# Value and gate projection of a gated recurrence: three products of 256 columns per weight block become one of 512 and one of 256

## The chip, the cores and the metric

The kernel runs on one core of one Trainium2 chip. A core has five engines that run their own instruction queues side by side: TensorE (PE in the profile; its weight loads are listed apart as PEld), VectorE (DVE), ScalarE (ACT), GpSimd (POOL) and SyncE (SP), which here issues most of the DMAs. The metric is the time of one execution on the device in microseconds (us). The kernel before takes 2153.63 us, the median of three runs (2153.37 to 2154.8 us).

## The reference, cut to what matters

The program is a two-layer decoder trunk on 1024 tokens of width 1024, all in float32: a gated linear recurrence (HGRN2) with 8 heads of 128, a gated convolutional feed-forward block, sliding-window attention, and a second feed-forward block. The change is in the first part alone. Of it the reference computes

```python
q, f, i, g = jnp.split(h @ w_in, 4, axis=-1)          # each (B, S, 1024): 8 heads of 128
fg = lb + (1.0 - lb) * jax.nn.sigmoid(heads(f))
o = hgrn2_chunkwise(jax.nn.silu(heads(q)), 1.0 - fg, heads(i), jnp.log(fg))   # i is the value
o = o * lax.rsqrt(jnp.mean(jnp.square(o), -1, keepdims=True) + RMS_EPS)
o = o * g_norm_w * jax.nn.silu(heads(g))              # g is the output gate
```

The two products that matter here are the value `i` and the gate `g`: for each head, 1024 tokens by 1024 inputs by 2 x 128 columns. The gate is used as g times sigmoid(g).

## The kernel before, in words

**Products in three parts.** A float32 operand is held as a high part (rounded to the type fp32r that TensorE reads) and a low part (the rest). A product is made of three matmuls into one accumulating bank of PSUM: high by high, high by low, low by high. That is `mm3` (L193 to L197): the matmul of L194 has the high part of the stationary operand and the high part of the moving one, L195 the high part and the low part, L196 the low part and the high part. Each matmul loads its stationary operand anew. The activations, transposed, stand in `T` (index 0 the high, 1 the low part); the weights stand in slots of `HL`. `split_raw` (L180) makes a slot from a loaded tile `raw`: ScalarE casts the high part (L176), then the low part is a subtraction (L169), on VectorE unless said otherwise.

**Value and gate.** For head h, `ig_block(h, us, tp)` (L673) makes value and gate of two blocks of 128 tokens. `us` are two weight tiles, each with four blocks of 128 inputs by 256 columns (128 of value, 128 of gate), high and low part one after the other. `proj_tok` (L213) goes over the two token blocks and the eight input blocks: the activations are stationary (128 by 128), the weights move (256 columns), so that one bank of 512 columns holds value and gate of two token blocks. Then ScalarE takes the sigmoid of the gate (L681) and copies the value to SBUF (L682), and VectorE multiplies sigmoid and gate (L684), reading PSUM. The tiles `V` and `G` have two buffers each; the recurrence of head h uses those of head h - 1 as scratch (L932).

**Order of the work.** The instructions of all engines are put in order by hand in this stage. A small class `Order` keeps a model time `od.t` of TensorE (each `mm3` adds 3n/2365 us) and a model `od.v` of when VectorE is done. Work other than the projections is written as generators; `od.tick()`, called after each `mm3`, steps those that are due, and then lets `lay` (L1060) fill VectorE with low parts and with sums of feed-forward weights (L1108) as long as its model stands less than 1.5 us ahead. A head has eight slots: four of `qf` (L819; 24 matmuls of 512 columns each) and four of `ig_block`. `recur` (L848), the recurrence of one head, is spread over some 50 us of other work: elementwise updates on VectorE (L918 to L923), copies on ScalarE (L905, L906), and small bursts of matmuls (L200).

At the beginning of each slot, `slot_begin` (L1083) puts all low parts still waiting and all gate products still waiting (`soon`) into VectorE's queue. At its end, `slot_end` (L1112) issues the casts of the next weights and registers their low parts. So the low parts go into VectorE's queue right behind the cast that they need, and the gate products right behind their sigmoid. The weights that are loaded wait for a free one of three `raw` tiles, on SP's queue. PSUM has four banks for the projections (`psmm`) and two tiles of two banks for the recurrence (`psax`).

After head 7, TensorE goes on with the output projection (`out_part`, L297), for which `Y_to_T` splits the finished heads into `T`; the last steps of the last recurrence lie between.

Of the kernel before, what the change touches and what calls it, by code (L numbers as in the profile page):

```python
# [107 lines left out]
def trunk(ctx: ExitStack, tc: tile.TileContext, a: dict, out: bass.AP):  # L108
# [31 lines left out]
    def psmm():  # L140
        return mmp.tile([P, 512], F32, name="psmm")
# [511 lines left out]
    with tc.tile_pool(name="t", bufs=1, reuse_waits="tile") as raws, hgrn_pool as hp:  # L653
# [14 lines left out]
        def qf_split(raw, eng=None):  # L668
            return split_raw(raw, eng).rearrange("p h (k c) -> p h k c", k=KC)

        VG = {-1: tuple(hp.tile([P, NB, P], F32, name=n, bufs=2) for n in "VG")}

        def ig_block(h, us, tp, soon=None):  # L673
            if tp == 0:
                VG[h] = (hp.tile([P, NB, P], F32, name="V", bufs=2), hp.tile([P, NB, P], F32, name="G", bufs=2))
            V, G = VG[h]
            ps = psmm()
            proj_tok(us, tp, ps)
            pv = ps.rearrange("p (t g c) -> p t g c", t=2, g=2)
            ts = slice(2 * tp, 2 * tp + 2)  # L680
            nc.scalar.activation(G[:, ts, :], pv[:, :, 1, :], AF.Sigmoid)  # L681
            nc.scalar.copy(V[:, ts, :], pv[:, :, 0, :])  # L682
            def gate():
                nc.vector.tensor_tensor(G[:, ts, :], G[:, ts, :], pv[:, :, 1, :], op=ALU.mult)  # L684
                od.vec(0.4)

            if soon is None:
                gate()
            else:
                soon.append(od.later(1.2, gate))  # L690

        nc.gpsimd.memset(nhalf, -0.5)
        make_identity(nc, ident)
# [7 lines left out]
        with tc.tile_pool(name="ep", bufs=1, reuse_waits="tile") as ep:  # L701
            pr = ep.tile([17, P], F32, name="pr")

            def x_load(tb):
                nc.sync.dma_start(Y[:, tb, :], x[tb * P:(tb + 1) * P, :])

            def x_block(tb):
                ps = psax()
                for kc in range(KC):
                    tr(ps[:, kc * P:(kc + 1) * P], Y[:, tb, kc * P:(kc + 1) * P])  # L710
                ts = slice(tb * P, (tb + 1) * P)
                split(T[:, 0, :, ts], T[:, 1, :, ts], ps.rearrange("p (k t) -> p k t", k=KC))

            def x_pair(tb):
                yield 0.0
                x_block(tb)
                yield 0.5
                x_block(tb + 1)

            warm = sm.tile([P, 1], F32, name="warm")  # L720
            mf = hp.tile([P, 7 * BL + P], F32, name="kd")
            nc.gpsimd.dma_start(pr[:16, :], a["hgrn_lb_logits"].rearrange("r (k p) -> (r k) p", p=P))
            nc.gpsimd.dma_start(pr[16:17, :], a["hgrn_gnorm_w"])
            with tc.manual_schedule(engines={EN.PE, EN.SP, EN.Activation, EN.DVE}):
                nc.scalar.activation(warm, nhalf, AF.Exp)
                x_load(0)
                raw0 = ig_load(0, 0)
                raw1 = ig_load(0, 1)
                for tb in range(1, 4):
                    x_load(tb)  # L730
                us = [ig_split(raw0, nc.gpsimd)]
                lm = ep.tile([P, NH], F32, name="lm")
                le = ep.tile([P, 2, NH], F32, name="le")

                idle = psmm()
                for n in (13, 40):
                    for _ in range(n):
                        nc.tensor.transpose(idle[:, :P], ident, ident)  # L738
                    if n == 13:
                        x_block(0)  # L740
                us.append(ig_split(raw1))

                def x_first():
                    yield 0.0
                    x_block(1)
                    yield 2.2
                    x_block(2)
                    yield 0.5
                    x_block(3)

                def lower_bounds():
                    yield 0.0
                    ps = psmm()
                    nc.tensor.transpose(ps[:, :17], pr, ident[:17, :17])
                    nc.vector.tensor_copy(par, ps[:, :17])
                    nc.vector.tensor_tensor(lm, par[:, 0:8], par[:, 8:16], op=ALU.max)
                    for r in range(2):
                        nc.vector.tensor_tensor(le[:, r, :], par[:, 8 * r:8 * r + 8], lm, op=ALU.subtract)
                    nc.scalar.activation(le, le, AF.Exp)
                    nc.scalar.activation(warm, nhalf, AF.Sigmoid)  # L760
                    nc.vector.tensor_tensor(lm, le[:, 0, :], le[:, 1, :], op=ALU.add)
                    nc.vector.reciprocal(lm, lm)
# [6 lines left out]
                od.finish([ahead, bounds])  # L769
                for tb in range(4, 6):  # L770
                    x_load(tb)
                raws0 = {"f": qf_load(0, 1)}
                for tb in range(6, NB):
                    x_load(tb)
                raws0["q"] = qf_load(0, 0)
                nc.sync.dma_start(mf, a["masks"])
                w0 = {}
                for tp in range(1, NB // 2 - 1):
                    ahead = od.spawn(x_pair(2 * tp + 2), 2.0)
                    ig_block(0, us, tp)  # L780
                    od.finish([ahead])
                w0["f"] = qf_split(raws0["f"])
                ig_block(0, us, NB // 2 - 1)
                w0["q"] = qf_split(raws0["q"])
                nc.vector.tensor_copy(msk, mf)

        def conv_params():
# [60 lines left out]
        def recur(h, qs, fg, kp):  # L848
# [80 lines left out]
            nc.vector.tensor_tensor(r0, qs, kp, op=ALU.mult)  # L929
            nc.vector.tensor_tensor(qp, qs, fg, op=ALU.mult)  # L930
            od.vec(4.4)
            idle = [t.rearrange("p c d -> p (c d)") for t in VG[h - 1]]  # L932
            r1 = idle[1][:, :S // 2]
            nc.vector.tensor_tensor(r1, kp[:, 0::2], qp[:, 1::2], op=ALU.mult)
            update(0)
            r2 = hp.tile([P, 2, S // 4, 2], F32, name="kd")
# [5 lines left out]
            early = stash(2, idle[0])  # L942
            yield od.behind(0.0, 0.5)
            update(2)
            yield od.behind(0.6, 2.1)
# [41 lines left out]
            yield 2.2  # L987
            while values_in[0] < h:
                yield 0.2
            V, G = VG[h]  # L990
            ps = psax()
            for c in range(NB - 1):
                cs = slice(c * P, (c + 1) * P)
# [12 lines left out]
            for c in range(NB):  # L1006
                cs = slice(c * P, (c + 1) * P)
                mm32(ps[:, cs], A[:, c, :], V[:, c, :], stop=c == 0)
                if c:
                    mm32(ps[:, cs], qp[:, cs], St[:, c, :], start=False)  # L1010
            og = hp.tile([P, NB, P], F32, name="og")
            pv = ps.rearrange("p (c t) -> p c t", c=NB)
            nc.vector.tensor_tensor(og, pv, G, op=ALU.mult)
# [36 lines left out]
        pending, soon, lowparts, movelows = [], [], [], []  # L1050

        def lay_low():
            lowparts.pop(0)[1]()
# [26 lines left out]
                movelows.append((tp, od.t + 1.4, lows[0]))  # L1080
                yield 2.6

        def slot_begin():  # L1083
            while lowparts:
                lay_low()
            od.finish(soon)
            soon.clear()
            slot_no[0] += 1
            n = slot_no[0]
            while summed and summed[0][2] < n:  # L1090
# [19 lines left out]
                pending.append(lambda i=i, r=r, last=last: (last(), summed.append((i, r, slot_no[0]))))  # L1110

        def slot_end(wait, *makes):  # L1112
            lows = []
            for make in makes:
                make(lows)
            for i, low in enumerate(lows):
                lowparts.append((od.t + wait + 1.0 * i, low))

        values_in, values_done, normed = [0], [-1], []
# [8 lines left out]
        with tc.manual_schedule(engines={EN.PE, EN.SP, EN.Activation, EN.DVE, EN.Pool}):  # L1128
# [23 lines left out]
            for h in range(1, NH):  # L1152
# [18 lines left out]
                for tp in range(NB // 2):  # L1171
                    if tp == lead[h]:
                        ready.append((h, w["out"]))
                    slot_begin()
                    if h == NH - 1 and tp:
                        moved.append(od.spawn(moves(tp - 1), 0.8))
                        if tp == 1:
                            oraw.append(load(out_loads(rows1, 0, (6, 7))))
                    ig_block(h, us, tp, soon)
                    slot_end(2.0, *make_w[tp])  # L1180
                values_in[0] = h
                if ready:
                    raise ValueError("a head has not begun")
                w = nw
# [1 line left out]
                raise ValueError("a unit is left")  # L1186
            while lowparts:
                lay_low()
            od.finish([params] + moved[:2] + soon)
            moved.append(od.spawn(moves(NB // 2 - 1), 3.0))  # L1190
            us = out_us
            begun = []
# [343 lines left out]
```

## Time and profile before

| | |
|---|---|
| median of three runs | 2153.63 us |
| the profiled execution | 2152.34 us |
| its span, first to last instruction | 2150.6 us |
| granted TensorE clock, mean | 0.999 |
| TensorE matmuls, busy | 2136.6 us, 13188 matmuls |
| VectorE, busy | 1742.7 us |
| ScalarE, busy | 918.3 us |

The span is that of one profiled execution; the time around it is 1.74 us. A row of a group of instructions gives line, engine, operation, output and inputs, the array tile and the shape, the count, then the busy time and the mean nanoseconds of one, and after the second bar the idle time of the engine just before them with what ended it. Matmuls are pipelined: one begins before the one ahead has ended, so the mean of one (287 ns for 256 columns) is longer than the distance from start to start, and it is this distance that tells what a matmul costs. A row of the timeline begins with its start and its length in us.

The recurrence stage is the first 500 us of the span or so. Heads 0 to 7 follow each other at some 54 us.

### The profile page before, as it was taken

The numbers are of one execution on the slowest core, as the hardware profiler recorded it, in microseconds if no ns is written. First come the engines' busy times: TensorE is split into PE (matmuls) and PEld (weight loads), VectorE is DVE, ScalarE is ACT, GpSimd is POOL, SyncE is SP. The second block draws the span as 40 slices with busy tenths as digits, with TensorE's granted clock in tenths as the row PEclk, the third lists the DMA queues.
The fourth block names the chain that finished last, engine by engine and source line by source line (L and its number), as shares of the span: only waits on it lengthen the run. The fifth ranks groups of instructions, "written<-read, shape, count | busy, mean of one in ns | idle before, by whom it ended". The sixth has DMA issues, their size and how long they took to land.

```text
span 2150.6 us, 33102 instructions
## 1 busy us (share of the span) xinstructions
PE 2136.6 (99%) x13188; PEld 1810.8 (84%) x13188; DVE 1742.7 (81%) x2316; ACT 918.3 (43%) x1473; POOL 120.8 (6%) x143
## 2 busy tenths in 40 slices
PE   9999999999999999999999999999999999999998
PEld 8899999998888888888888888878888888888887
DVE  3877665577999998988978558969999999878986
ACT  3344434353444444434433256743544444444430
POOL 1000000000100000000001123311000000000002
PEclk9999999999999999999999999999999999999999
DMA  5765541123223222228854411133233222249662
GB/s 200 274 217 201 192 138 31 44 72 136 99 80 96 89 89 79 79 98 276 286 186 157 128 28 32 33 118 108 89 98 98 82 85 89 78 142 332 227 214 89
DMA packets 229842, 279.03 MB, mean 130 GB/s; under 512 B 29960, under 2 KB 158648, under 8 KB 226872
## 3 DMA queue, kind: packets, MB, share of 16 engines
q1 hardware_dynamic: 228736, 276.53, 38.6%
q8 instruction: 103, 1.69, 0.3%
q10 hardware_dynamic: 856, 0.37, 0.1%
q14 instruction: 51, 0.42, 0.1%
q0 software_dynamic: 96, 0.02, 0.0%
HBM read 213.94 MB, written 62.94 MB: 129 GB/s over the span
## 4 chain that ended last, share of the span: by engine, by line
PE 95%; DVE 3%; issue 1%; ACT 0%; DMA 0%; POOL 0%; DVEq 0%; ACTq 0%; POOLq 0%; SPq 0%
PE psmm L194 20%; PE psmm L196 19%; PE psmm L195 19%; PE psax L194 9%; PE psax L195 9%; PE psax L196 9%; PE psax L200 3%; PE psmm L200 1%; PE psax L204 1%; PE psmm L204 1%; PE psax L1330 1%; DVE Y L473 1%; PE psmm L738 0%; DVE T L169 0%; DVE TX L169 0%
## 5 line engine op out<-in xcount | busy, mean ns | idle before, releaser
L194 PE MATMUL psmm<-T,HL 128*128 128x512 f32 x768 | 305.0, 397 | 0.0
L195 PE MATMUL psmm<-T,HL 128*128 128x512 f32 x768 | 299.3, 390 | 0.0
L196 PE MATMUL psmm<-T,HL 128*128 128x512 f32 x768 | 299.3, 390 | 0.0
L473 DVE SCALAR_TENSOR_TENSOR Y<-Y,cwt 128x1023 f32<-128x1023 f32 (+1 forms) x176 | 225.1, 1281 | 41.3 <-ACT Y L471 39.5
L221 ACT CAST HL<-rx 128x1024 fp32r<-128x1024 f32 (+1 forms) x151 | 151.7, 1008 | 199.8 <-PE psmm L195 47.1
L194 PE MATMUL psmm<-HL,T 128*128 128x256 f32 (+1 forms) x656 | 197.2, 301 | 0.0
L196 PE MATMUL psmm<-HL,T 128*128 128x256 f32 (+1 forms) x656 | 194.3, 296 | 0.3 <-DVE T L169 0.3
L195 PE MATMUL psmm<-HL,T 128*128 128x256 f32 (+1 forms) x656 | 194.1, 296 | 0.0
L169 DVE TENSOR_TENSOR HL<-rx,HL 128x1024 fp32r<-128x1024 f32 (+1 forms) x151 | 174.6, 1162 | 13.9 <-ACT HL L221 13.8
L196 PEld LDWEIGHTS psmm<-T,HL 128*128 128x128 f32 x768 | 144.1, 188 | 30.9
L194 PEld LDWEIGHTS psmm<-T,HL 128*128 128x128 f32 x768 | 144.4, 188 | 28.8
L195 PEld LDWEIGHTS psmm<-T,HL 128*128 128x128 f32 x768 | 144.5, 188 | 27.7
L471 ACT ACTIVATE Y<-Y,cwt 128x1024 f32<-128x1024 f32 x88 | 109.0, 1238 | 99.4 <-DVE Y L460 91.4
L194 PE MATMUL psax<-T,HL 128*128 128x512 f32 x352 | 137.3, 390 | 0.0
L196 PE MATMUL psax<-T,HL 128*128 128x512 f32 x352 | 137.0, 389 | 0.0
L195 PE MATMUL psax<-T,HL 128*128 128x512 f32 x352 | 137.0, 389 | 0.0
L196 PEld LDWEIGHTS psmm<-HL,T 128*128 128x128 f32 x656 | 125.2, 191 | 4.0 <-DVE T L169 0.8
L194 PEld LDWEIGHTS psmm<-HL,T 128*128 128x128 f32 x656 | 125.3, 191 | 3.7 <-issue 0.4
L195 PEld LDWEIGHTS psmm<-HL,T 128*128 128x128 f32 x656 | 125.4, 191 | 3.3
L243 POOL TENSOR_TENSOR rs<-rs,nhalf 128x1 f32<-128x1 f32 x32 | 45.0, 1406 | 1398.9 <-DVE rs L242 1398.9
L169 DVE TENSOR_TENSOR HL<-raw,HL 128x1024 fp32r<-128x1024 f32 x51 | 62.5, 1227 | 72.0 <-ACT HL L176 71.8
L221 ACT CAST HT<-rx 128x1024 fp32r<-128x1024 f32 (+1 forms) x37 | 35.5, 961 | 111.2 <-DVE rx L427 74.4
(298 smaller groups left out, 5106.1 us busy)
## 6 DMA issues: line engine op xcount, KB each, us to landing
rx<-in_ffn_w_in_dram SPq DMA_DIRECT2D x136, 256.0 KB, 3.2
rx<-gd SPq DMA_DIRECT2D x118, 256.0 KB, 3.9
Y<-in_ffn_w_out_dram SPq DMA_DIRECT2D x44, 512.0 KB, 5.9
bsd<-Y SPq DMA_DIRECT2D x22, 1024.0 KB, 4.8
gd<-Y SPq DMA_DIRECT2D x44, 512.0 KB, 2.6
rx<-in_ffn_w_out_dram SPq DMA_DIRECT2D x54, 256.0 KB, 4.2
R<-bsd SPq DMA_DIRECT2D x44, 256.0 KB, 4.9
Y<-in_ffn_w_in_dram SPq DMA_DIRECT2D x40, 256.0 KB, 3.0
```

Source lines behind the costliest of these rows:

```text
L169: make = lambda e: e.tensor_tensor(lo, src, hi.bitcast(F32), op=ALU.subtract)
L194: nc.tensor.matmul(ps, st(0), mv(0), start=start, stop=False)
L195: nc.tensor.matmul(ps, st(0), mv(1), start=False, stop=False)
L196: nc.tensor.matmul(ps, st(1), mv(0), start=False, stop=stop)
L200: nc.tensor.matmul(ps, lhsT, rhs, start=start, stop=stop, **kw)
L204: nc.tensor.transpose(ps, src, ident)
L221: nc.scalar.copy(hi, src)
L243: nc.gpsimd.tensor_tensor(rs, rs, nhalf, op=ALU.pow)
L471: nc.scalar.activation(c, u, AF.Identity, bias=cwt[:, l, 3, ci:ci + 1], scale=cwt[:, l, 2, ci:ci + 1])
L473: nc.vector.scalar_tensor_tensor(c[:, sh:], u[:, :S - sh], cwt[:, l, 2 - sh, ci:ci + 1], c[:, sh:], op0=ALU.mult, op1=ALU.add)
L1330: nc.tensor.matmul(pv[:, e, jj, lo:], q[bp // 2][es, e, qs], Kl[es, pp, ks] if low else Kh[:, pp, e, ks], start=not low and jj == 0, stop= ...
```

## The change

`ig_block` takes one token block per bank. For each of the eight input blocks it issues one matmul with the high part of the activations stationary, and the high and the low part of the weights moving as one operand of 512 columns (two runs of 256, 1024 words apart), so that high by high gathers in the first half of the bank and high by low in the second half; then one matmul of 256 columns with the low part of the activations stationary, into the first half. So there are two matmuls and two weight loads where there were three, with as many columns in all. The model time of the group becomes 0.347 us.

A new generator `values` empties a bank: ScalarE copies the second half to SBUF, VectorE adds the first half to it; after every second token block ScalarE takes the sigmoid of two blocks' gates from SBUF into a new tile `sg`, and VectorE multiplies. Value and gate stand in one tile `VG` with the two side by side.

`slot_begin` no longer lays low parts and gate products. A new function `rest`, called at the beginning of `slot_end`, lays the low parts that are left from the slot before, and finishes the `values` (and query products) that were already waiting one slot earlier. So low parts are laid when VectorE's model has room and they are due, one slot later at most. The value of head h counts as present when the addition of its last block is in the queue.

```diff
+        VG = {-1: hp.tile([P, NB, 2, P], F32, name="VG", bufs=2)}
+        values_in, soon, gated = [-1], [], {}
+
+        def values(h, tb, ps):
+
+            vg = VG[h][:, tb]
+            nc.scalar.copy(vg, ps[:, 256:].rearrange("p (g c) -> p g c", g=2))
+            yield 0.9
+            nc.vector.tensor_tensor(vg, vg, ps[:, :256].rearrange("p (g c) -> p g c", g=2), op=ALU.add)
+            od.vec(0.45)
+            if tb == NB - 1:
+                values_in[0] = h
+            if tb % 2:
+                G = VG[h][:, tb - 1:tb + 1, 1, :]
+                sg = hp.tile([P, 2, P], F32, name="sg")
+                yield 0.7
+                nc.scalar.activation(sg, G, AF.Sigmoid)
+                yield 0.8
+                nc.vector.tensor_tensor(G, G, sg, op=ALU.mult)
+                od.vec(0.4)
...
-            ps = psmm()
-            proj_tok(us, tp, ps)
-            pv = ps.rearrange("p (t g c) -> p t g c", t=2, g=2)
-            ts = slice(2 * tp, 2 * tp + 2)
-            nc.scalar.activation(G[:, ts, :], pv[:, :, 1, :], AF.Sigmoid)
-            nc.scalar.copy(V[:, ts, :], pv[:, :, 0, :])
...
+            for tb in (2 * tp, 2 * tp + 1):
+                ps, ts = psmm(), slice(tb * P, (tb + 1) * P)
+                for kc in range(KC):
+                    w = us[kc // 4]
+                    nc.tensor.matmul(ps, T[:, 0, kc, ts], w[:, :, kc % 4, :], start=kc == 0, stop=False)
+                    nc.tensor.matmul(ps[:, :256], T[:, 1, kc, ts], w[:, 0, kc % 4, :], start=False, stop=kc == KC - 1)
+                    od.t += 0.347
+                    od.tick()
+                soon.append(od.spawn(values(h, tb, ps)))
+                gated.setdefault(h, []).append(soon[-1])
+                od.tick()
+
+        def soon_all(left=0):
+            while len(soon) > left:
+                od.finish([soon.pop(0)])
...
-            idle = [t.rearrange("p c d -> p (c d)") for t in VG[h - 1]]
-            r1 = idle[1][:, :S // 2]
+            idle = VG[h - 1].rearrange("p c g d -> p (c g d)")
+            r1 = idle[:, S:S + S // 2]
...
-            V, G = VG[h]
+            V, G = VG[h][:, :, 0, :], VG[h][:, :, 1, :]
...
+            od.finish(gated[h])
             og = hp.tile([P, NB, P], F32, name="og")
...
-        def slot_begin():
+        def rest():
             while lowparts:
                 lay_low()
-            od.finish(soon)
-            soon.clear()
+            od.finish(old)
+            soon[:] = [t for t in soon if t[1] is not None]
+            old[:] = soon
+
+        def slot_begin():
             slot_no[0] += 1
...
         def slot_end(wait, *makes):
+            rest()
             lows = []
...
                         if tp == 1:
+                            rest()
                             oraw.append(load(out_loads(rows1, 0, (6, 7))))
-                    ig_block(h, us, tp, soon)
+                    ig_block(h, us, tp)
                     slot_end(2.0, *make_w[tp])
-                values_in[0] = h
...
-            od.finish([params] + moved[:2] + soon)
+            soon_all()
+            od.finish([params] + moved[:2])
```

In head 0, `soon_all(1)` stands behind each pair of token blocks.

More of the change, by code (lines that the diff above doesn't have):

```diff
@@ L669, in qf_split @@
             return split_raw(raw, eng).rearrange("p h (k c) -> p h k c", k=KC)
-        VG = {-1: tuple(hp.tile([P, NB, P], F32, name=n, bufs=2) for n in "VG")}
-        def ig_block(h, us, tp, soon=None):
-            if tp == 0:
-                VG[h] = (hp.tile([P, NB, P], F32, name="V", bufs=2), hp.tile([P, NB, P], F32, name="G", bufs=2))
-            V, G = VG[h]
-            ps = psmm()
-            proj_tok(us, tp, ps)
-            pv = ps.rearrange("p (t g c) -> p t g c", t=2, g=2)
-            ts = slice(2 * tp, 2 * tp + 2)
[L681 to L690, printed above, removed]
+        VG = {-1: hp.tile([P, NB, 2, P], F32, name="VG", bufs=2)}
@@ new lines, in ig_block @@
+        def ig_block(h, us, tp):
+            if tp == 0:
+                VG[h] = hp.tile([P, NB, 2, P], F32, name="VG", bufs=2)
+            for tb in (2 * tp, 2 * tp + 1):
[9 more added lines that the diff above has]
+                od.tick()
@@ L769, in trunk @@
                 od.finish([ahead, bounds])
+                soon_all(1)
                 for tb in range(4, 6):
@@ L781, in trunk @@
                     od.finish([ahead])
+                    soon_all(1)
                 w0["f"] = qf_split(raws0["f"])
@@ L941, in recur @@
             update(1)
-            early = stash(2, idle[0])
+            early = stash(2, idle[:, :S])
             yield od.behind(0.0, 0.5)
@@ L989, in recur @@
                 yield 0.2
-            V, G = VG[h]
+            V, G = VG[h][:, :, 0, :], VG[h][:, :, 1, :]
             ps = psax()
@@ L1049, in trunk @@
         slot_no = [-1]
-        pending, soon, lowparts, movelows = [], [], [], []
+        pending, lowparts, movelows, old = [], [], [], []
         def lay_low():
@@ L1117, in slot_end @@
                 lowparts.append((od.t + wait + 1.0 * i, low))
-        values_in, values_done, normed = [0], [-1], []
+        values_done, normed = [-1], []
         wo = a["hgrn_w_out"][0]
@@ L1188, in trunk @@
                 lay_low()
-            od.finish([params] + moved[:2] + soon)
+            soon_all()
+            od.finish([params] + moved[:2])
             moved.append(od.spawn(moves(NB // 2 - 1), 3.0))
```

## The prediction

> **What bounds the kernel.** I read the page first, then the waits of TensorE in the stage of the change, then its timeline for the distance between matmuls.
>
> ```profile
> span 2150.6 us, 33102 instructions
> PE 2136.6 (99%) x13188; PEld 1810.8 (84%) x13188; DVE 1742.7 (81%) x2316; ACT 918.3 (43%) x1473; POOL 120.8 (6%) x143
> ...
> PE   9999999999999999999999999999999999999998
> ...
> PE 95%; DVE 3%; issue 1%; ACT 0%; DMA 0%; POOL 0%; DVEq 0%; ACTq 0%; POOLq 0%; SPq 0%
> ```
>
> The chain that ended last is 95% TensorE, and its busy slices are full from the first to the last but one. Busy alone could hide waits, so here is who TensorE waited for in the first 560 us, which hold the whole recurrence:
>
> ```profile
> PE psmm L738 <- POOL ident masks.py:199: 2.8, 1, 2.8
> PE psmm L196 <- DVE T L169: 0.3, 1, 0.3
> ```
>
> Two waits, both before 16 us. So in this stage time is what TensorE's instructions take, and anything that only relieves VectorE or ScalarE is worth nothing.
>
> What does a matmul take? Start to start, from the timeline of TensorE: 256 columns between two projections, and 512 columns in a `qf` slot.
>
> ```profile
> 322.40 0.40 PE L196 MATMUL psmm<-T,HL 128*128 128x512 f32 x1
> 322.63 0.28 PE L194 MATMUL psmm<-HL,T 128*128 128x256 f32 x1
> ...
> 324.06 0.28 PE L194 MATMUL psmm<-HL,T 128*128 128x256 f32 x1
> ...
> 329.94 0.28 PE L195 MATMUL psmm<-HL,T 128*128 128x256 f32 x1
> ```
>
> ```profile
> 305.15 0.39 PE L196 MATMUL psmm<-T,HL 128*128 128x512 f32 x1
> ...
> 308.55 0.39 PE L196 MATMUL psmm<-T,HL 128*128 128x512 f32 x1
> ```
>
> ```profile
> 289.72 0.28 PE L196 MATMUL psmm<-HL,T 128*128 128x256 f32 x1
> 289.84 0.40 PE L194 MATMUL psmm<-T,HL 128*128 128x512 f32 x1
> ```
>
> From 324.06 to 329.94 are 49 steps: 0.120 us each. From 305.15 to 308.55 are 15 steps: 0.2267 us each. The change alternates the two, and both junctions are there: behind a 512 the next 256 starts after 0.23 us, behind a 256 the next 512 starts after 0.12 us. If a matmul costs a + b N, then a = 2 x 120 - 226.7 = 13.3 ns, whatever its columns. That fixed part is what the change can save.
>
> **The change part by part.**
>
> *The products.* There are 8 heads x 8 token blocks x 8 input blocks = 512 groups, which the rows by line confirm (576 matmuls of 256 columns per line of `mm3`; 64 of them belong to the shared value projection of the attention layer, 4 calls of 16):
>
> ```profile
> L194 PE MATMUL psmm<-HL,T 128*128 128x256 f32 x576 | 165.3, 287 | 0.0
> ```
>
> A group is now 3 x 0.120 = 0.360 us and becomes 0.2267 + 0.120 = 0.3467 us. Gain: 512 x 13.3 ns = 6.8 us. What no row shows is a 512-column operand in two runs of 256. It is bounded by 0.2267 us (one run) and 0.240 us (as if two matmuls, which makes the gain nil); I take 0.2267, since the stream is still of 512 words and one instruction, and keep 0.240 for a rival. A gain beyond 6.8 us is excluded by the columns, which stay 768 per group.
>
> The Trainium skill, "TensorE: Matmul & The Clock Gate", section "Back-to-back issue gap", gives a warm gap of N / 2.4 + 2.5 ns, that is a fixed part of 2.5 ns and not 13.3; by it a group would save 2.5 ns and the change an estimated 1.3 us. The trace does not agree: by that rule 256 columns would take 109 ns, and the rows have 120.
>
> *The start.* Head 0 waits for the transposed input:
>
> ```profile
> 15.34 0.28 PE L195 MATMUL psmm<-HL,T 128*128 128x256 f32 x1
> 15.96 0.39 PE L196 MATMUL psmm<-HL,T 128*128 128x256 f32 x1 [0.33 <-DVE T L169]
> ```
>
> The second token block cannot go on before that low part, so what the first token block saves (8 x 13.3 ns = 0.1 us) is lost in this wait. Take 0.1 us off.
>
> *VectorE and ScalarE.* Rows by line of 24 to 464 us:
>
> ```profile
> L169 DVE TENSOR_TENSOR HL<-raw,HL 128x1024 fp32r<-128x1024 f32 x34 | 41.5, 1224 | 67.1 <-ACT HL L176 67.1
> L684 DVE TENSOR_TENSOR G<-G,psmm 128x256 f32<-128x256 f32 x31 | 12.9, 416 | 21.8 <-ACT V L682 21.8
> L681 ACT ACTIVATE G<-psmm 128x256 f32<-128x256 f32 x30 | 11.5, 382 | 59.4 <-PE psmm L196 59.4
> L682 ACT COPY V<-psmm 128x256 f32<-128x256 f32 x30 | 11.1, 369 | 0.0
> ```
>
> The 32 gate products and 32 sigmoids stay; 64 copies replace 32, so ScalarE gets 32 x 0.369 = 11.8 us more; VectorE gets 64 additions of 0.416 = 26.6 us more, 3.3 us per head. Both lie beside TensorE if there is room. The windows of the fullest and of a later head:
>
> ```profile
> 76.00:130.00 54.00, 54.00 (x646) 49.08 (x648) 45.12 (x79) 22.59 (x51) 2.82 (x2) 1.00 0.72 259
> ...
> 351.00:404.00 53.00, 53.00 (x686) 48.36 (x680) 28.73 (x51) 22.34 (x49) 1.83 (x2) 1.00 0.14 41
> ```
>
> The third busy column is VectorE: 45.1 and 28.7 us of some 54, so 3.3 us more fit, even in the fullest head. ScalarE (22 us) has room. And moving the low parts from the slot's beginning to when they are due takes the 67.1 us away in which VectorE stood at the head of its queue for a cast. Its worth is nil, as TensorE did not wait, but it is the cover for the additions.
>
> *New waits.* The addition waits for ScalarE's copy, the sigmoid for the addition, the product for the sigmoid. Behind the sigmoid on ScalarE stand the recurrence's copies and the casts; behind the product on VectorE stand the updates. TensorE's small bursts wait for those. Their margin in head 5 and in head 7:
>
> ```profile
> 300.95 0.69 DVE L920 TENSOR_TENSOR kp<-kp,tot 128x512 f32<-128x512 f32 x1
> ...
> 303.94 0.20 PE L200 MATMUL psax<-qp,kp 128*32 128x32 f32 x1
> ```
>
> ```profile
> 463.54 0.68 DVE L920 TENSOR_TENSOR kp<-kp,tot 128x512 f32<-128x512 f32 x1
> 463.72 0.74 PE L200 MATMUL psax<-kd 128*32 128x16 f32 x64
> ...
> 464.28 0.70 PE L200 MATMUL psax<-qp,kp 128*32 128x32 f32 x32
> ```
>
> In head 5 the update ended 303.94 - 301.64 = 2.3 us ahead of the matmul that reads it; in head 7, whose recurrence lies wholly among `ig_block` slots, 0.06 us. There one addition in front (0.42 us) makes TensorE wait. The model clock adds to it: it counted 0.325 us for a group of 0.360 us, so a planned pause of 2.1 us was 2.3 us long; now 0.347 stands for 0.347 and the 0.2 us are gone. Bounds: nothing, since in head 7 a block of VectorE goes as well,
>
> ```profile
> 453.81 1.23 DVE L169 TENSOR_TENSOR HL<-raw,HL 128x1024 fp32r<-128x1024 f32 x1 [3.92 <-ACT HL L176]
> ```
>
> and 5 bursts x 0.42 = 2.1 us. I take one addition, 0.4 us, nearest to the only point without margin.
>
> *The end of the stage.* The last recurrence's output must be in `T` when the output projection comes to its last input block:
>
> ```profile
> 496.86 0.48 DVE L226 SCALAR_TENSOR_TENSOR T<-psax,par,T 128x256 fp32r<-128x256 f32 x1 [6.62 <-ACT T L225]
> ```
>
> ```profile
> 501.60 0.39 PE L194 MATMUL psmm<-HL,T 128*128 128x512 f32 x1
> ```
>
> 497.34 against 501.60: 4.3 us of slack, which holds whatever head 7 loses above. Nil.
>
> *SP's queue and PSUM.* A low part that comes up to a slot later frees its `raw` tile later, and SP's loads wait for exactly that:
>
> ```profile
> SPq L164 <- DVE HL L169: 110.3, 10, 23.2
> ```
>
> ```profile
> L176 ACT CAST HL<-raw 128x1024 fp32r<-128x1024 f32 x34 | 35.7, 1052 | 0.1
> ```
>
> The casts that need those loads stood idle for 0.1 us in all between 24 and 464 us, so a delay of up to one slot (some 5.5 us) stays hidden; without that cover each head would pay the part beyond the slack. A bank is now filled in 8 x 0.347 = 2.8 us and needed again four banks, 11 us, after its filling began; copy and addition take 0.8 us and their planned pause 0.9. Nil. One layout for value and gate moves no work.
>
> **Sum.** 6.8 - 0.1 - 0.4 = 6.3 us, against the profiled execution's 2152.34 us (span 2150.6 and 1.7 around it): 2146.0 us. The median of the runs stands 1.3 us above that execution, so I predict 2147.3 us. About 0.2%, 4.3 us, is what a measurement can tell from no change.
>
> **The rivals.**
>
> *The second run costs like a second matmul* (0.240 us for the 512 columns). For it: no row has this shape. Against it: one instruction, one weight load. The gain is nil: 2153.6 us, with the 0.4 us of waiting 2154.0. No change. Chance 0.08.
>
> *The fixed part is not per matmul.* If most of the 13.3 ns went with something that stays (the bank's accumulation, or the 256 columns), only a few ns per group would be saved; taking one fifth of it, for a number, 512 x 2.7 ns = 1.4 us, 2152.2 us. Against it: 512 columns take 226.7 ns and not 240. No change. Chance 0.04. This is where the rule of the Trainium skill ("TensorE: Matmul & The Clock Gate", "Back-to-back issue gap") would put it.
>
> *VectorE's additions cost TensorE a little in every head*: two bursts per head late by 0.25 us, 16 x 0.25 = 4 us. For it: the margin of 0.06 us in head 7. Against it: 2.3 us in head 5. 2153.6 - 6.7 + 4 = 2150.9 us. No change. Chance 0.10.
>
> *Slower: VectorE falls behind for good.* If additions and products, each chained to ScalarE, make the updates late by two additions (0.83 us) at two bursts in each head, TensorE pays 16 x 0.83 = 13.3 us: 2153.6 - 6.7 + 13.3 = 2160.2 us. It decides from 0.69 us at each of the 16 points (11 us). For it: the fullest head would have VectorE busy 48 of 54 us. Against it: later heads have 20 us to spare, and the 67.1 us of blocked queue go. Chance 0.08.
>
> **How the numbers follow.** The forecast has 0.70; its own range is 2145.5 (no wait at all, 2146.8, less the 1.3 us by which one execution differed) to 2149.0 (the 2.1 us bound of waits). The range of 8 in 10 goes on to 2153.2: it takes in the third rival and the second, and leaves out the first and the slower one with the forecast's edges. Faster 0.70; same 0.08 + 0.04 + 0.10 = 0.22; slower 0.08.
>
> **What would show it.** In the changed profile: 512 matmuls of 256 columns less per line of `mm3` and 1024 new ones under two lines of `ig_block`; within a slot their starts 0.227 and 0.120 us apart in turn; TensorE's waits in the first 560 us still under 1 us; VectorE's wait for the cast (67.1 us) mostly gone; VectorE busy some 27 us more; everything behind 500 us earlier by 6 us and unchanged. The prediction is wrong if the 512-column starts are 0.235 us or more apart, or if waits of the small bursts (L200) for VectorE or ScalarE add up to more than 2 us.

## The result, and the profile after

| | before | changed |
|---|---|---|
| median of 22 runs each | 2153.3 us (2152.07 to 2154.8) | 2156.46 us (2154.74 to 2159.88) |
| ratio, 95% interval | | 1.0015 [1.0009, 1.002] |
| profiled execution, its span | 2152.34 us, 2150.6 us | 2154.74 us, 2153.0 us |

The changed kernel is 3.2 us slower; 2147.3 us was predicted, and the range ended at 2153.2 us. The difference is small, but its interval excludes 1. The profiled execution of the changed kernel is the fastest of its 22 and 1.7 us below their median, so its rows can account for 2.4 us of span and not for the whole 3.2.

The page of the changed kernel: the span, the busy times, the chain that ended last by engine, and the two new groups of matmuls.

```profile
span 2153.0 us, 32150 instructions
PE 2134.6 (99%) x12676; PEld 1784.1 (83%) x12676; DVE 1764.1 (82%) x2380; ACT 933.0 (43%) x1505; POOL 119.5 (6%) x143
...
PE 98%; DVE 1%; ACT 0%; issue 0%; POOL 0%; DVEq 0%; ACTq 0%; POOLq 0%
...
L699 PE MATMUL psmm<-HL,T 128*128 128x512 f32 x512 | 182.8, 399 | 0.0
L700 PE MATMUL psmm<-HL,T 128*128 128x256 f32 x512 | 143.5, 280 | 0.4 <-DVE T L169 0.4
```

The change is there: 512 matmuls fewer (12676 instead of 13188), TensorE busy 2.0 us less, and yet the span is 2.4 us longer. TensorE still bounds the kernel, so the time must lie between its instructions. TensorE's waits in the first 560 us, as for the kernel before (line waited on, engine and line that ended the wait; us in total, times, longest):

```profile
PE psmm L196 <- DVE T L169: 3.9, 1, 3.9
PE psmm L757 <- POOL ident masks.py:199: 2.8, 1, 2.8
PE psmm L194 <- issue: 0.6, 1, 0.6
PE psmm L700 <- DVE T L169: 0.4, 1, 0.4
```

One wait is new, of 3.9 us, and it is a matmul of `mm3` that needs a low part of `T` from VectorE. TensorE's timeline at that place (start, length):

```profile
464.59 0.39 PE L195 MATMUL psmm<-HL,T 128*128 128x512 f32 x1
468.86 0.78 PE L196 MATMUL psmm<-HL,T 128*128 128x512 f32 x1 [3.89 <-DVE T L169]
469.44 0.63 PE L194 MATMUL psmm<-HL,T 128*128 128x512 f32 x1
469.86 0.63 PE L195 MATMUL psmm<-HL,T 128*128 128x512 f32 x1
```

These are the first matmuls of the output projection (`out_part`). Its 15th, the third of input block 4, reads the low half of `T` for token block 0, head 4. Without a wait it starts 0.23 us behind its neighbour; here 4.27 us pass. That is a stop of 4.0 us, and behind it the matmuls are 0.42 us apart and not 0.23. What VectorE and then ScalarE did meanwhile, from their timelines:

```profile
464.71 1.22 DVE L169 TENSOR_TENSOR HL<-raw,HL 128x1024 fp32r<-128x1024 f32 x1
466.61 0.42 DVE L679 TENSOR_TENSOR VG<-VG,psmm 128x256 f32<-128x256 f32 x1 [0.68 <-ACT VG L677]
467.51 0.43 DVE L689 TENSOR_TENSOR VG<-VG,sg 128x256 f32<-128x256 f32 x1 [0.48 <-ACT sg L687]
467.86 4.09 DVE L169 TENSOR_TENSOR T<-Y,T 128x768 fp32r<-128x768 f32 x4
```

```profile
449.31 0.83 ACT L221 CAST T<-Y 128x768 fp32r<-128x768 f32 x1
...
466.20 0.37 ACT L677 COPY VG<-psmm 128x256 f32<-128x256 f32 x1
467.06 0.42 ACT L687 ACTIVATE sg<-VG 128x256 f32<-128x256 f32 x1 [0.49 <-DVE VG L679]
```

The high part of that block was cast at 449.31, so the low part could have been laid from 450.1 on. It was laid at 467.86, as the first of four. Ahead of it in VectorE's queue stood a low part of the output weights, which TensorE does not need yet, and then the chain of the last `values`: copy on ScalarE, addition, sigmoid on ScalarE, product. VectorE stood idle in that chain for 0.68 and 0.48 us with the low part that TensorE waited for right behind it. In the code, the low parts of `T` (`movelows`) have the last rank in `lay`, and behind head 7 `while lowparts: lay_low()` and `soon_all()` come ahead of them. The same stretch in windows, 16 us from 464 (span of the window, busy us with count of TensorE, its weight loads, VectorE, ScalarE and GpSimd, granted clock, DMA share, GB/s), first before, then after:

```profile
464.00:480.00 16.00, 16.00 (x194) 13.71 (x183) 12.64 (x26) 7.26 (x15) 0.00 (x0) 1.00 0.21 71
```

```profile
464.00:480.00 16.00, 12.11 (x85) 9.76 (x84) 8.59 (x16) 6.17 (x12) 0.00 (x0) 0.89 0.00 0
```

A full engine has become one that stands for 3.9 us, and the granted clock fell. A narrower window holds just the stretch in which it did:

```profile
468.91:472.33 3.42, 3.42 (x32) 2.58 (x34) 3.04 (x3) 0.00 (x0) 0.00 (x0) 0.50 0.00 0
```

Half the clock for 3.4 us is 1.7 us of TensorE's work. So the stop costs 4.0 + 1.7 = 5.7 us by these rows.

Everything later is as before. The matmul that the prediction took for the end of the stage, at 501.60 us before, now starts here:

```profile
503.93 0.39 PE L194 MATMUL psmm<-HL,T 128*128 128x512 f32 x1
```

From it to the end of the span are 2153.0 - 503.93 = 1649.1 us, and before 2150.6 - 501.60 = 1649.0 us. The difference of the two spans can be laid out piece by piece with the first matmul of the projections, first before, then after:

```profile
11.40 0.36 PE L194 MATMUL psmm<-HL,T 128*128 128x256 f32 x1
```

```profile
12.01 0.48 PE L699 MATMUL psmm<-HL,T 128*128 128x512 f32 x1
```

The start is 0.6 us later. The 15th matmul of the output projection started at 468.23 us before (its row stands in the part on why the prediction was wrong); without its stop it would now start at 464.59 + 0.23 = 464.82. From the first projection to it were 456.8 us and would be 452.8: the eight heads became 4.0 us shorter. The stop adds 4.0 us. From the 15th matmul to the one at the end of the stage were 33.4 us and are 35.1, which is the 1.7 us of low clock. With 0.1 us behind it, 0.6 - 4.0 + 4.0 + 1.7 + 0.1 = 2.4 us, as the spans differ.

### The profile page after: what moved, and what is told of

It is laid out like the page before. It is cut to its first block, busy times and chain, and to the rows that moved or that the text cites. A ratio compares the mean times of both kernels' runs of the same rounds, so it can differ in the third digit from the quotient of the medians.

```text
span 2153.0 us, 32150 instructions
## 1 busy us (share of the span) xinstructions
PE 2134.6 (99%) x12676; PEld 1784.1 (83%) x12676; DVE 1764.1 (82%) x2380; ACT 933.0 (43%) x1505; POOL 119.5 (6%) x143
## 4 chain that ended last, share of the span: by engine, by line
PE 98%; DVE 1%; ACT 0%; issue 0%; POOL 0%; DVEq 0%; ACTq 0%; POOLq 0%
PE psmm L194 17%; PE psmm L196 17%; PE psmm L195 17%; PE psax L194 9%; PE psax L195 9%; PE psax L196 9%; PE psmm L699 5%; PE psax L200 3%; PE psmm L700 3%; PE psmm L204 1%; PE psmm L200 1%; PE psax L204 1%; PE psax L1358 1%; PE psmm L757 0%; DVE Y L473 0%
## 5 line engine op out<-in xcount | busy, mean ns | idle before, releaser
L699 PE MATMUL psmm<-HL,T 128*128 128x512 f32 x512 | 182.8, 399 | 0.0
L700 PE MATMUL psmm<-HL,T 128*128 128x256 f32 x512 | 143.5, 280 | 0.4 <-DVE T L169 0.4
L699 PEld LDWEIGHTS psmm<-HL,T 128*128 128x128 f32 x512 | 96.1, 188 | 21.4
L700 PEld LDWEIGHTS psmm<-HL,T 128*128 128x128 f32 x512 | 96.7, 189 | 1.2 <-DVE T L169 0.9
L195 PEld LDWEIGHTS psax<-T,HL 128*128 128x128 f32 x352 | 66.1, 188 | 13.6
L196 PEld LDWEIGHTS psax<-T,HL 128*128 128x128 f32 x352 | 66.1, 188 | 13.6
```

The lines of the kernel that those rows point to most:

```text
L195: nc.tensor.matmul(ps, st(0), mv(1), start=False, stop=False)
L196: nc.tensor.matmul(ps, st(1), mv(0), start=False, stop=stop)
L699: nc.tensor.matmul(ps, T[:, 0, kc, ts], w[:, :, kc % 4, :], start=kc == 0, stop=False)
L700: nc.tensor.matmul(ps[:, :256], T[:, 1, kc, ts], w[:, 0, kc % 4, :], start=False, stop=kc == KC - 1)
```

## The experiments

The theory from these rows: the products save a few us as meant, and the new queue rule (`rest`, `soon_all`) loses more by laying the low part of `T` too late. The rivals: that the products save nothing, and that the additions make VectorE late whatever the rule is. Four kernels ran on one chip, with 33 runs of the kernel before at a median of 2153.5 us.

### Lay that one low part early

In the changed kernel, ahead of the last pair of token blocks of head 7:

```diff
+                    if h == NH - 1 and tp == NB // 2 - 1:
+                        while movelows and movelows[0][0] == 0:
+                            lay_moved()
                     ig_block(h, us, tp)
```

> The changed kernel, with one addition: before the last pair of token blocks of head 7, VectorE's queue gets the low parts of the activations of tokens 0 to 255 that the output projection will read first. Theory A (the products did get cheaper, and the loss is one stop of TensorE of 4.0 us behind head 7 plus some 2 us of low clock after it): the stop is gone, some 6 us less than the changed kernel, about 2150.3 us, 0.14% less than before. Theory B (the additions on VectorE and ScalarE cost TensorE a little everywhere, and the stop only absorbs slack that would be lost later): the time stays within 1.5 us of the changed kernel, 2155 us or more.

Measured: 2150.42 us (2148.6 to 2151.64, 11 runs), ratio to the kernel before 0.9985 [0.9976, 0.9994]. VectorE's timeline and TensorE's waits in the first 560 us of this kernel:

```profile
455.38 0.95 DVE L169 TENSOR_TENSOR T<-Y,T 128x768 fp32r<-128x768 f32 x1
```

```profile
PE psmm L757 <- POOL ident masks.py:199: 2.8, 1, 2.8
PE psmm L194 <- issue: 0.5, 1, 0.5
PE psmm L700 <- DVE T L169: 0.4, 1, 0.4
```

The low part is laid 12.5 us earlier, the wait of 3.9 us is gone and no other has come. Nothing else was edited, and the kernel is 6.0 us faster than the changed one, as the first theory had it. It is also 3.1 us faster than the kernel before, with an interval below 1: the rest of the change is worth something.

### The products as three matmuls again

In the kernel with the early low part, the 512 columns as two matmuls of 256, with the same order of everything and the same model time:

```diff
-                    nc.tensor.matmul(ps, T[:, 0, kc, ts], w[:, :, kc % 4, :], start=kc == 0, stop=False)
+                    nc.tensor.matmul(ps[:, :256], T[:, 0, kc, ts], w[:, 0, kc % 4, :], start=kc == 0, stop=False)
+                    nc.tensor.matmul(ps[:, 256:], T[:, 0, kc, ts], w[:, 1, kc % 4, :], start=False, stop=False)
```

> As e1_low_early, but the 512-column matmul is issued as two of 256 (high by high into the first half of the bank, high by low into the second), so three matmuls and three weight loads per group as before the change; all else, the model time too, is the same. What the change of the products is worth by itself is this time less that of e1_low_early. By the prediction's start-to-start distances 512 x 13.3 ns = 6.8 us, so about 2157 us; by the sums of starts in the changed trace (182.7 against 187.4 us) 4.7 us, about 2155 us; by a fixed part of 2.5 ns per matmul 1.3 us, about 2151.6 us.

Measured: 2155.31 us (2154.14 to 2157.89, 11 runs), ratio 1.0009 [1.0, 1.0018]. So the merged products are worth 2155.31 - 2150.42 = 4.9 us, 9.6 ns for each of the 512 groups: the rival that they save nothing is out, and the 13.3 ns of the prediction were too much. The two traces say the same: over the 476 groups behind which the next one follows within 0.45 us, the mean distance from group to group is 363.4 ns here and 353.8 ns with the early low part alone. Against the kernel before, this one has the additions, the new rule and the new layout but not the merged products, and it is 1.8 us slower, with an interval that just reaches no change. The one long wait from 24 to 560 us:

```profile
PE psax L200 <- issue: 1.3, 1, 1.3
```

It is ended by nothing that the profile shows, and its cause stays open. Whether the other executions have such a stop is not known: the profiled one, at 2154.14 us, is the fastest of the 11.

### The old rule with the new products

In the changed kernel `slot_begin` gets its old lines back, and the two calls of `rest` go:

```diff
         def slot_begin():
+            while lowparts:
+                lay_low()
+            od.finish(soon)
+            soon.clear()
             slot_no[0] += 1
...
         def slot_end(wait, *makes):
-            rest()
             lows = []
...
-                            rest()
                             oraw.append(load(out_loads(rows1, 0, (6, 7))))
```

> The changed kernel with the old rule for the queue: low parts and the rest of the value chains are put into VectorE's queue at the beginning of each slot, not a slot later. Theory A1 (the additions fill VectorE near head 7, so the low parts of lowest rank come late whatever the rule): the stop in front of the first output projection remains, 3 us or more, and the time is 2155 us or more. Theory A2 (it is the new rule that lets the value chain of the last block stand in front of them): the stop is below 1 us and the time near 2150 to 2151 us.

Measured: 2157.48 us (2155.84 to 2159.24, 10 runs), ratio 1.0018 [1.0009, 1.0027]. The old rule does not bring the time back. Neither theory is met: the stop in front of the output projection shrinks to 1.3 us, and the time is still lost, at other places. TensorE's waits in the first 560 us (those of the changed kernel at the start left out) and the window from 464 us:

```profile
PE psax L200 <- DVE kp L942: 2.7, 2, 1.6
PE psax L204 <- DVE og L1052: 1.4, 1, 1.4
PE psmm L196 <- DVE T L169: 1.3, 1, 1.3
PE psmm L699 <- DVE VG L679: 1.0, 1, 1.0
PE psax L200 <- ACT kd L928: 0.4, 1, 0.4
```

```profile
464.00:480.00 16.00, 13.14 (x180) 10.33 (x179) 15.38 (x30) 10.14 (x19) 0.00 (x0) 1.00 0.00 1
```

At the end of head 7 VectorE is all but full: busy 15.38 of 16 us, with TensorE down to 13.14. The delay is spread over five kinds of wait, 6.8 us in all, of which 3.1 us are those that the prediction feared: the recurrence's small bursts (L200) waiting for VectorE or ScalarE. The longest of them, 1.6 us at 459.66, comes ahead of this window, and VectorE was not full there; it had stood for a cast at the head of its queue:

```profile
455.87 1.23 DVE L169 TENSOR_TENSOR HL<-raw,HL 128x1024 fp32r<-128x1024 f32 x1 [2.75 <-ACT HL L176]
```

Such waits for casts are 65.2 us from 24 to 480 us in this kernel, as in the kernel before (67.1). So the rival that the additions make VectorE late fits here, under the old rule only, where these waits stay. The new rule removes these waits and makes one of its own; the two kernels (2157.48 and 2156.46 us) cannot be told apart by these runs.

### The new rule alone

The kernel before with nothing of the change but the rule: `rest` with its list `old`, called where the change calls it, and the three lines out of `slot_begin`.

```diff
-        pending, soon, lowparts, movelows = [], [], [], []
+        pending, soon, lowparts, movelows, old = [], [], [], [], []
...
-        def slot_begin():
+        def rest():
             while lowparts:
                 lay_low()
-            od.finish(soon)
-            soon.clear()
+            od.finish(old)
+            soon[:] = [t for t in soon if t[1] is not None]
+            old[:] = soon
+
+        def slot_begin():
...
         def slot_end(wait, *makes):
+            rest()
```

> The kernel before with only the new rule for the queue (low parts and gate products up to a slot later), without the new products and additions. The prediction put this at nothing, as TensorE did not wait: 2153.3 us within 0.7 us, no stop of TensorE above 1 us. If the new rule by itself makes the low parts of the output projection late, a stop of some us shows near 465 us and the time is 2156 us or more.

Measured: 2158.45 us (2157.56 to 2159.71, 10 runs), ratio 1.0024 [1.0015, 1.0034]: 5.0 us slower than the kernel before. TensorE's and VectorE's timelines of this kernel, and the window in which the clock was low:

```profile
467.82 0.39 PE L195 MATMUL psmm<-HL,T 128*128 128x512 f32 x1
471.12 0.80 PE L196 MATMUL psmm<-HL,T 128*128 128x512 f32 x1 [2.91 <-DVE T L169]
```

```profile
469.77 0.42 DVE L684 TENSOR_TENSOR G<-G,psmm 128x256 f32<-128x256 f32 x1 [2.09 <-ACT V L682]
470.11 2.96 DVE L169 TENSOR_TENSOR T<-Y,T 128x768 fp32r<-128x768 f32 x3
```

```profile
470.53:473.94 3.41, 2.82 (x7) 2.15 (x7) 3.41 (x5) 0.28 (x1) 0.00 (x0) 0.50 0.00 0
```

The same matmul stops, with no addition and no merged product in the kernel: VectorE waits 2.09 us for ScalarE with the last gate product at the head of its queue and the low part of `T` behind it. The sizes agree within the interval: the rows give 3.30 - 0.23 = 3.1 us of stop and half of the 2.82 us in which TensorE worked at the low clock, 1.4 us, together 4.5 us, and 5.0 us were measured (3.2 to 7.3 us by the interval of the ratio).

### Keep TensorE busy through the stop

This and the three kernels behind it ran in a second set, with 33 runs of the kernel before at a median of 2153.52 us. Here it is the changed kernel with 36 transposes, whose output nobody reads, two matmuls ahead of the one that stops; the low part comes no sooner.

```diff
-                begun.append(psmm())
+                if tb != 1:
+                    begun.append(psmm())
...
-                out_part(begun[tb], us, tb, range(KC - 1))
+                if tb == 0:
+                    begun.append(psmm())
+                    out_part(begun[0], us, 0, range(4))
+                    for _ in range(36):
+                        nc.tensor.transpose(begun[1][:, :P], ident, ident)
+                    out_part(begun[0], us, 0, range(4, KC - 1))
+                else:
+                    out_part(begun[tb], us, tb, range(KC - 1))
```

> The changed kernel with 36 transposes that nobody reads, some 3.9 us of TensorE's time, put in front of the matmul that stops for 4.0 us. The stop itself cannot shrink, as the low part comes no sooner, but TensorE does not idle. If the rest of the loss (6.0 us between the changed kernel and e1_low_early, less 4.0 of stop) is the granted clock, which stood at one half for 3.4 us after the stop, it goes: about 2154.5 us, and no stretch of half clock near 470 us. If the clock plays no part: 2156.5 us.

Measured: 2153.25 us (2152.72 to 2154.73, 10 runs), ratio 1.0 [0.9991, 1.0009]. TensorE's timeline and the window from 464 us:

```profile
463.72 4.09 PE L1231 MATMUL psmm<-ident 128*128 128x128 f32 x36
...
468.23 0.50 PE L196 MATMUL psmm<-HL,T 128*128 128x512 f32 x1
```

```profile
464.00:480.00 16.00, 16.00 (x131) 13.92 (x130) 10.08 (x18) 5.58 (x10) 0.00 (x0) 1.00 0.00 1
```

The clock stays at 1.00, and the kernel is 2156.46 - 2153.25 = 3.2 us faster for doing 36 useless instructions. Over all executions it is the same: the mean granted clock is 0.999 in all ten here, and 0.997 or 0.998 in 21 of the 22 of the changed kernel. By the rows of the changed kernel the low clock costs 1.7 us, and the two profiled executions, 2154.74 and 2153.02 us, differ by 1.7 us too; the medians' intervals, some 1 to 2 us each way, do not tell 1.7 from 3.2. That the low clock costs something is shown, its size only to that.

### The rule with the early low part, and the early low part alone

Both in the kernel before: with the new rule, and without it as a control. The edit is that of the first experiment, behind a sort by token pair:

```diff
+                    if h == NH - 1 and tp == NB // 2 - 1:
+                        movelows.sort(key=lambda m: m[0])
+                        while movelows and movelows[0][0] == 0:
+                            lay_moved()
```

> e4_policy_alone (the kernel before with only the new rule) with the low parts of tokens 0 to 255 put into VectorE's queue before the last pair of token blocks of head 7. If the late low parts are all that the new rule costs: 2153.5 us within 0.7 us, no stop near 468 us. If the rule costs elsewhere too: 2155 us or more.

> The kernel before with only these low parts put forward. A control: if laying them early is a gain by itself and not just the repair of the stop, it shows here. Expected by theory A: no change, 2153.5 us within 0.7 us, as TensorE does not wait for them in the kernel before.

Measured: 2153.38 us (2152.27 to 2154.85, 10 runs) with the rule, 2153.65 us (2151.78 to 2154.29, 10 runs) without; the ratios are 1.0 [0.999, 1.0009] and 1.0 [0.9991, 1.0009]. So what the rule costs the kernel before, 5.0 us, is this one late low part, up to the 2 us that the interval leaves. The early low part gains nothing where nobody waits for it, which means that the 3.1 us of the first experiment are not its gift but the change's.

### The 512 columns in one run

In the kernel with the early low part, each block's high and low weights are laid side by side, so that the operand is 512 words in one run and not two runs of 256:

```diff
...
-                    nc.tensor.matmul(ps, T[:, 0, kc, ts], w[:, :, kc % 4, :], start=kc == 0, stop=False)
+                    nc.tensor.matmul(ps, T[:, 0, kc, ts], w[:, kc % 4, :, :].rearrange("p h c -> p (h c)"), start=kc == 0, stop=False)
...
```

> e1_low_early with high and low part of a weight block side by side in the slot, so that the 512-column operand is one run of 512 words and not two of 256. If the two runs are why a pair of matmuls takes 353 ns in some slots and not 347 (and the products gave 4.9 us and not 6.8): starts 227 and 120 ns apart everywhere and about 2148.5 us. If the runs are nothing: the same two patterns of starts and 2150.4 us within 0.7 us.

Measured: 2149.81 us (2148.79 to 2152.42, 11 runs), ratio 0.9985 [0.9977, 0.9994], not told from the 2150.42 us of two runs. Its timeline shows, as that of the changed kernel does, two distances between pairs:

```profile
99.68 0.40 PE L704 MATMUL psmm<-HL,T 128*128 128x512 f32 x1
...
101.80 0.40 PE L704 MATMUL psmm<-HL,T 128*128 128x512 f32 x1
...
105.86 0.40 PE L704 MATMUL psmm<-HL,T 128*128 128x512 f32 x1
...
113.15 0.39 PE L704 MATMUL psmm<-HL,T 128*128 128x512 f32 x1
```

From 99.68 to 101.80 are 6 pairs of 0.353 us, from 105.86 to 113.15 21 pairs of 0.347 us. The two runs of the operand are not what makes some pairs slower.

## Why the prediction was wrong

**What bounds the kernel: right.** TensorE is 98% of the chain, and only what stands between its instructions counts.

**The products: right mechanism, wrong size.** 6.8 us were forecast, 4.9 us measured (the kernel with three matmuls). TensorE's timeline of the changed kernel, in two slots:

```profile
107.08 0.40 PE L699 MATMUL psmm<-HL,T 128*128 128x512 f32 x1
107.31 0.28 PE L700 MATMUL psmm<-HL,T 128*128 128x256 f32 x1
...
112.97 0.39 PE L699 MATMUL psmm<-HL,T 128*128 128x512 f32 x1
```

```profile
209.24 0.40 PE L699 MATMUL psmm<-HL,T 128*128 128x512 f32 x1
...
214.18 0.40 PE L699 MATMUL psmm<-HL,T 128*128 128x512 f32 x1
```

From 107.08 to 112.97 are 17 pairs of 0.3465 us, just the 0.3467 of the prediction, and the junctions are 0.23 and 0.12 us as read from the kernel before. From 209.24 to 214.18 are 14 pairs of 0.353 us. The gain per group is 13.5 ns in the one and 7.1 ns in the other, and 9.6 ns on the whole. So the step that was too large was to take 0.3467 us for every group. The Trainium skill ("TensorE: Matmul & The Clock Gate", "Back-to-back issue gap") gives the rule that the prediction weighed, N / 2.4 + 2.5 ns, for a matmul by itself and not for a stream with weight loads, which the prediction left out; by it the change would have saved an estimated 1.3 us. The 4.9 us measured lie nearer to the rows than to the rule. The rival of a second run that costs like a second matmul is refuted twice, by these starts and by the layout with one run.

**The start: not to be read from one execution.** The forecast was 0.1 us; the wait for the low part stayed (0.4 us on L700). The first projection's matmul starts at 11.40 us in one profile and at 12.01 in the other. In the two traces the records of the full clock begin at 6.87 and at 8.11 us, and half of the 1.24 us between them is that 0.6 us: in these two executions the clock rose at different moments.

**VectorE and ScalarE: right.** VectorE is busy 21.4 us more (1742.7 to 1764.1) where 26.6 were counted, ScalarE 14.7 us more (918.3 to 933.0) where 11.8 were. The rows by line of 24 to 464 us:

```profile
L169 DVE TENSOR_TENSOR HL<-raw,HL 128x1024 fp32r<-128x1024 f32 x33 | 40.1, 1219 | 14.7 <-ACT HL L176 14.7
...
L679 DVE TENSOR_TENSOR VG<-VG,psmm 128x256 f32<-128x256 f32 x62 | 25.6, 416 | 11.9 <-ACT VG L677 11.9
...
L689 DVE TENSOR_TENSOR VG<-VG,sg 128x256 f32<-128x256 f32 x31 | 13.1, 424 | 8.6 <-ACT sg L687 8.6
```

An addition takes 0.416 us, as taken. The wait for casts fell from 67.1 to 14.7 us; additions and products stand 11.9 + 8.6 us for ScalarE, where the products stood 21.8 us. The prediction called that wait the cover for the additions, and the old rule with the new products bears that out: there the waits for casts stay and the bursts wait.

**New waits in head 7: none** where they were looked for (0.4 us forecast). L200 waits for nobody in the changed kernel; both rivals built on late updates (2150.9 and 2160.2 us) are refuted for it.

**The end of the stage: here it failed.** "Nil" was argued from one consumer alone, the last recurrence's output at 501.60 us with 4.3 us of slack. But the output projection begins some 37 us earlier and reads the other low parts of `T`, and the prediction never asked when these are laid. It said of the rule that its worth is nil, as TensorE did not wait, and took that to hold for its cost too. A rule that lets things in a queue be laid later also puts something else ahead of what has the last rank; that this was the next thing TensorE needed was to be seen in the code (`lay`, and the two lines behind head 7), and how near it was in the profile of before. There VectorE lays the same low part, and TensorE's 15th matmul reads it, at

```profile
465.29 0.98 DVE L169 TENSOR_TENSOR T<-Y,T 128x768 fp32r<-128x768 f32 x1
```

```profile
468.23 0.39 PE L196 MATMUL psmm<-HL,T 128*128 128x512 f32 x1
```

that is with 468.23 - 466.27 = 2.0 us to spare: one more low part of the weights (1.22 us) and two additions (0.42 us each) in front of it, or the wait of 2.09 us for ScalarE seen above, and it is late. The new rule alone cost 5.0 us, and 6.0 us were lost in the changed kernel.

**The sum by the experiments**: +1.8 (additions, rule and layout with three matmuls, against the kernel before; the interval reaches 0) - 4.9 (the products) + 6.0 (the late low part) = +2.9 us, where 3.2 were measured. These three are steps from one median to the next, so they add up to the measured difference whatever the causes are, and prove nothing by it; the causes rest on the rows and on the single edits. The pieces of the profiled executions above agree with two of them on their own: the heads became 4.0 us shorter, where the products were worth 4.9, and stop and low clock took 5.7 us, where the early low part gave 6.0. The 1.8 us are unexplained. Nothing in the rivals of the prediction held this case: the slower one had the right sign for another reason.

## What to carry to other kernels

When a change lets work in a queue be done later, list what stands behind it in that queue, the last-ranked first, and for each item the consumer that comes next on the engine that bounds the kernel, beyond the stage that is changed. A saving of 9.6 ns times 512, 4.9 us, is lost by a single stop of 4.0 us with 1.7 us of low clock behind it, so the margins at the seams between stages deserve as much reading as the loop. And a slower result may hide a good change: one item laid early turned +3.2 us into -3.1 us.

## What the hardware showed

- A stop of TensorE can cost more than its length. In the changed kernel and with the new rule alone the granted clock fell to 0.50 for 3.4 us; in the former the next matmuls stood 0.42 us apart and not 0.23. It fell at 468.91 us in the one, as the stop of 3.89 us ended, and at 470.53 us in the other, 2.3 us after the last matmul (467.82 + 0.39 = 468.21) had ended. The waits of up to 1.6 us in the kernel with the old rule left the clock at 1.00, and transposes in place of idling did too. The Trainium skill ("TensorE: Matmul & The Clock Gate", "What's actually happening") says that the clock falls to half after an idle window of about 3.4 us and comes back after as long a busy one. The half and the 3.4 us of low clock agree; that 2.3 us of idling were enough in one run does not.
- A stream of alternating 512- and 256-column matmuls ran in some stretches at 0.347 and in others at 0.353 us per pair, with either layout of the operand; what puts a stretch in the one or the other is open.
